# Folding the low rows of light experts by a 128-row product, and scattering their down projection unfolded

## The chip, the cores and the metric

One NeuronCore of a Trainium2 chip runs the whole program. The metric is the device time of one execution in microseconds; the time before is the median of three runs, 1436.17 us (1435.22 to 1437.19).

## The reference

A two-layer decoder trunk over 256 tokens of width 1024. Each layer has a mixer (window attention beside a state-space branch), then a feed-forward part: dense in the first layer, a mixture of experts in the second. The change touches the mixture alone.

```
def _swiglu(h, wg, wu, wd):
    return (jax.nn.silu(h @ wg) * (h @ wu)) @ wd

logits = x2d @ w_router                      # 256 tokens, 8 experts
top_v, top_i = lax.top_k(logits, 2)
gates = softmax(top_v)
# for each expert e, over the tokens that chose it:
#     y[tok] += _swiglu(x2d[tok], wg[e], wu[e], wd[e]) * gate
# widths: 1024 -> 3584 -> 1024
```

All values are float32.

## The kernel before

**Precision.** TensorE multiplies in a reduced 32-bit form. So each operand is split into a high part and the rest (`wh` and `wl` of a weight tile `w`, by ScalarE and then VectorE), and a product is the sum of several partial ones that accumulate in one bank of PSUM.

**Experts.** The eight experts are sorted by the number of their tokens. The four largest ("heavy", places 0 to 3) get 128 rows; the four smallest ("light", places 4 to 7) get `ROOM` = 64 rows. They run alternately, in the order 0, 4, 1, 5, 2, 6, 3, 7 (`TURNS`, line 30). Each expert has `NCH` = 7 chunks of 512 hidden columns, and each chunk loads 12 weight tiles of 512 KB: 4 for the gate, 4 for the up projection, 4 for the way down. A weight tile serves two products of 512 columns for each pair of parts.

**Heavy experts** (`glu_up`, `glu_down`) use three partial products: high x high, high x low, low x high.

**Light experts** (`light_up`, `light_down`) have at most 64 rows, so their high and low parts stand side by side in one 128-column set of weights: columns 0 to 63 are the high part, 64 to 127 the low part. Two products (with `wh` and with `wl`) then leave the sum for the high part in rows 0 to 63 of the bank and the one for the low part in rows 64 to 127. The result is the sum of the two halves. `join` (line 1407) forms it: ScalarE copies rows 64 to 127 to the tile `low`, and TensorE adds them to rows 0 to 63 by a product with `shift`, a 64x64 identity that lies in rows 64 to 127 of the place matrix tile `PTl`. A light chunk has two joins in the up projection (gate and up bank). After the last chunk of a light expert, `scatter_light` (line 1518) joins the two accumulators as well.

**From tokens to rows and back.** `gather_light` (line 1357) makes, for all light experts at once, the selection `PPl` (tokens by rows), uses it to pick the rows, and transposes it to the place matrix `PTl` (rows by tokens). `scatter` and `scatter_light` split an expert's result into `yh` and `yl` and hand them to `give` (line 1532), which multiplies the place matrix with both and adds the outcome, times the gate, to the residual `X`. The last expert is a light one, so its `scatter_light` and `give` are the end of the kernel: each half of `X` leaves for memory as soon as it is updated.

**Order.** The operations are recorded first, with the tiles that they read and write. A planner (`Plan.order`, line 240) then lays them out by list scheduling with costs written in the code, and the program is emitted in that order: each engine works through its own list, and weight loads stay in the order in which they were recorded. Buffers come in pools: 44 of 128x1024 (`m`: weight tiles, their splits, `yh`, `yl`, `PTl`), 8 of 128x512 (`h`: `low`, `sg`, `hth`, selections, place matrices), small ones (`s`), and 8 PSUM banks. A weight tile is loaded when a buffer of the first pool comes free, so products that end release loads. In the trace every operation has line 445, where they are emitted; they are told apart by their tiles, written as output, then inputs: `bank<-low,PTl` is the product of a join.

**The expert sort** (`sort`, line 1260) uses a 128x64 scratch tile `big` in the small pool, up to the two calls of `placed` that sort slots and gates.

Of the kernel before, what the change touches and what calls it, by code (L numbers as in the profile page):

```python
# [447 lines left out]
class Kernel:  # L448
# [811 lines left out]
    def sort(self, msk, ones):  # L1260

        nc, tt, ts, stt = self.nc, self.tt, self.ts, self.stt
        K = self.K
        bank = self.bank()
        for t in range(2):
            nc.tensor.matmul(bank[:, 0:8], ones, msk[:, 8 * t:8 * t + 8], start=t == 0, stop=t == 1)
        rows = self.S(8, "rows")
        nc.vector.tensor_copy(rows, bank[:, 0:8])
        key = self.S(8, "key")
        stt(key, rows, 8.0, K[:, CK:CK + 8], OP.mult, OP.add)  # L1270
        inner = lambda x: x.unsqueeze(1).to_broadcast([128, 8, 8])
        outer = lambda x: x.unsqueeze(2).to_broadcast([128, 8, 8])
        square = lambda x: x.rearrange("p (a b) -> p a b", a=8)
        big = self.big = self.S(64, "big")
        tt(square(big), inner(key), outer(key), OP.is_gt)
        place = self.S(8, "place")
        nc.vector.tensor_reduce(place, square(big), AX.X, OP.add)

        self.perm = self.S(64, "perm")
        tt(square(self.perm), inner(place), outer(K[:, CT:CT + 8]), OP.is_equal)  # L1280
        tt(square(big), square(self.perm), inner(K[:, CT:CT + 8]), OP.mult)
        at = self.S(8, "pi")
        nc.vector.tensor_reduce(at, square(big), AX.X, OP.add)
        ids = self.plan.buf("s", [128, 8], I32, "ids")
        nc.vector.tensor_copy(ids, at)
        self.known = len(self.plan.ops)
        self.plan.add("DMA", "registers", (None, ids, self.registers), {})
        self.sslot = self.placed(self.slot, "sslot")

        room = self.S(8, "room")  # L1290
        ts(room, place, float(HEAVY), float(128 - ROOM), OP.is_lt, OP.mult)
        ts(room, room, float(ROOM), None, OP.add)
        tt(rows, rows, room, OP.subtract)
        self.most = self.S(1, "most")
        nc.vector.tensor_reduce(self.most, rows, AX.X, OP.max)
        ts(self.most, self.most, 0.0, None, OP.max)
        self.over = self.S(16, "over")
        v = lambda x: x.rearrange("p (t e) -> p t e", t=2)
        tt(v(self.over), v(self.slot), room.unsqueeze(1).to_broadcast([128, 2, 8]), OP.subtract)
# [57 lines left out]
    def gather_light(self, hn):  # L1357

        nc = self.nc
        n = NE - HEAVY  # L1360
        m = n * ROOM
        PP = self.H("PPl", F32R)
        for t in range(2):
            for i in range(n):
                c, o = 8 * t + HEAVY + i, m * t + ROOM * i
                self.ts(PP[:, o:o + ROOM], self.K[:, CT:CT + ROOM], self.sslot[:, c:c + 1], None, OP.is_equal)
        h = [self.M("lx", F32R).rearrange("p (k e q m) -> p k e q m", k=2, e=n, q=2) for _ in range(4)]
        for b in range(4):
            bank = self.bank()
            for i in range(2):  # L1370
                k = 2 * b + i
                for j, x in enumerate(hn):
                    nc.tensor.matmul(bank[:, m * i:m * i + m], x[:, 128 * k:128 * k + 128], PP[:, m * (j // 2):m * (j // 2) + m], start=j == 0, stop=j == 3)
            for i in range(2):
                k = 2 * b + i
                hi, lo = (h[b][:, i, :, q] for q in range(2))
                v = bank[:, m * i:m * i + m].rearrange("p (e m) -> p e m", e=n)
                g = self.mg[:, k:k + 1]
                self.act(hi, v, AF.Copy, scale=g)
                self.stt(lo, v, g, hi.bitcast(F32), OP.mult, OP.subtract)  # L1380
        PT = self.M("PTl", F32R)
        for t in range(2):
            bank = self.bank()
            for i in range(n):
                o = m * t + ROOM * i
                nc.tensor.transpose(bank[0:ROOM, 128 * i:128 * i + 128], PP[:, o:o + ROOM].bitcast(F32), self.ident)
            nc.vector.tensor_copy(PT[0:ROOM, 512 * t:512 * t + 512], bank[0:ROOM])

        self.shift = PT[ROOM:128, 0:ROOM]
        nc.vector.tensor_copy(self.shift, self.ident[ROOM:128, ROOM:128])  # L1390
        bank = self.bank()
        for i in range(n):
            for t in range(2):
                o = m * t + ROOM * i
                nc.tensor.matmul(bank[0:ROOM, i:i + 1], PP[:, o:o + ROOM].bitcast(F32), self.rs[:, t:t + 1], start=t == 0, stop=t == 1)
        rs = self.S(4, "rsl")
        nc.vector.tensor_copy(rs[0:ROOM], bank[0:ROOM, 0:n])
        return PT[0:ROOM].rearrange("p (t e m) -> p t e m", t=2, e=n), lambda j, k: h[k // 2][:, k % 2, j].rearrange("p q m -> p (q m)"), rs[0:ROOM]

    def both(self, out, x, w, first):  # L1400

# [4 lines left out]

    def join(self, bank):

        low = self.H("low", F32R)[ROOM:128]
        self.act(low, bank[ROOM:128], AF.Copy)  # L1410
        self.nc.tensor.matmul(bank[0:ROOM], self.shift, low, start=False, stop=True, skip_group_check=True)
        return bank[0:ROOM]

    def light_up(self, src, of, rs):
# [31 lines left out]
    def moe(self, R):  # L1446
# [11 lines left out]
        for turn, j in enumerate(TURNS):  # L1458
            if j in GROUPS:
                self.plan.after = [mark] if j else []  # L1460
                got = self.gather(GROUPS[j], hn) if j < HEAVY else self.gather_light(hn)
                self.plan.after = []
                for n, i in enumerate(GROUPS[j]):
                    rows[i] = (n, *got)
            n, PT, of, rse = rows[j]
            acc = [self.bank(), self.bank()]
            for i in range(NCH):
                i == 0 and self.marks.append((f'e{j}', len(self.plan.ops) + 3))
                if i == self.gate_at - 1:
                    mark = len(self.plan.ops) + 1  # L1470
                if i == self.gate_at:
                    if j == 0:
                        hn = self.split_rows([mark])
                    mark = len(self.plan.ops) + 1
                if j:
                    w = [Late(lambda j=j, i=i, q=q: e[bass.ds(self.regs[j], 1), i, q].rearrange("o p n -> (o p) n")) for q in range(12)]
                else:
                    w = [e[0, i, q] for q in range(12)]
                self.ks = self.LEAN[1] if NCH * turn + i < self.LEAN[0] else self.KR[7]
                if j < HEAVY:  # L1480
                    ht = self.glu_up(w[:8], lambda t, k, n=n, of=of: of(n, k), 1, rse[:, n:n + 1])
                    down, scatter, to = self.glu_down, self.scatter, [acc]
                else:
                    ht = self.light_up(w[:8], lambda k, n=n, of=of: of(n, k), rse[:, n:n + 1])
                    down, scatter, to = self.light_down, self.scatter_light, acc

                if rest:
                    rest[0](*rest[1:])
                rest = (down, i, w[8:], ht, to, scatter(j, n, PT, acc) if i == NCH - 1 else None)
        rest[0](*rest[1:])  # L1490
        return hn

# [11 lines left out]
    def scatter(self, place, j, PT, acc):  # L1504

        y = []

        def half(h):
            if not y:
                y.extend((self.M("yh", F32R), self.M("yl", F32R)))  # L1510
            c = slice(512 * h, 512 * h + 512)
            self.act(y[0][:, c], acc[h], AF.Copy)
            self.tt(y[1][:, c], acc[h], y[0][:, c].bitcast(F32), OP.subtract)
            self.give(place, h, [[(PT[:, t, j], y[i][:, c]) for i in range(2)] for t in range(2)])

        return half

    def scatter_light(self, place, j, PT, acc):
        y = []

        def half(h):
            if not y:
                y.extend((self.M("yh", F32R), self.M("yl", F32R)))
            c = slice(512 * h, 512 * h + 512)
            a = self.join(acc[h])
            self.act(y[0][0:ROOM, c], a, AF.Copy)
            self.tt(y[1][0:ROOM, c], a, y[0][0:ROOM, c].bitcast(F32), OP.subtract)
            self.give(place, h, [[(PT[:, t, j], y[i][0:ROOM, c]) for i in range(2)] for t in range(2)])

        return half  # L1530

# [211 lines left out]
```

## Time and profile before

| | before |
|---|---|
| median of 3 runs | 1436.17 us |
| profiled execution, its own time | 1438.01 us |
| its span (first to last instruction) | 1436.0 us |
| TensorE busy | 1399.2 us, 97% |
| VectorE busy | 1204.7 us, 84% |
| ScalarE busy | 1013.6 us, 71% |
| DMA, mean rate | 294 GB/s |
| mean granted clock of TensorE | 0.989 |

The profile is of one execution. PE is TensorE's products and PEld its weight loads, which overlap; DVE is VectorE, ACT ScalarE, SP the engine that issues the loads. A busy TensorE is not one at its peak. The mixture takes roughly the second half: its loads start at about 412 us, the last of them lands at about 1410 us.

### The profile page before, as it was taken

What the parts mean: (1) busy time and instruction counts of PE and PEld (TensorE: products, weight loads), DVE (VectorE), ACT (ScalarE), POOL (GpSimd) and SP (SyncE); (2) the same over time, 40 slices, a digit from 0 to 9 for tenths busy, and PEclk for the clock granted to TensorE, in tenths of its full rate; (3) what the DMA queues carried; (4) which work ended last, traced back from release to release, by engine and by line L of the source; (5) the groups of instructions that cost most, each with busy time, mean ns of one, the idle gap of its engine ahead of it and who ended that gap; (6) DMA issues with size and microseconds to landing.
All of it is one profiled execution on the core that took longest, in us unless ns stands there. A gap on an engine that the chain in (4) does not pass through costs nothing.

```text
span 1436.0 us, 20731 instructions
## 1 busy us (share of the span) xinstructions
PE 1399.2 (97%) x6558; PEld 1070.7 (75%) x6558; DVE 1204.7 (84%) x1640; ACT 1013.6 (71%) x1322; POOL 25.4 (2%) x44
## 2 busy tenths in 40 slices
PE   7999999999999999999899999999999899999997
PEld 4888888888888878876678876678886667887554
DVE  7888994554695699899979999999898989998986
ACT  5586754445447387799778788988778778787775
POOL 3000110000000000000000000000000000000000
PEclk9999999999999899999999999999999999999999
DMA  6357155555447679699999999999999999999993
GB/s 218 106 171 241 57 163 191 177 189 187 140 147 258 241 235 375 219 363 383 357 354 382 383 392 363 394 348 393 378 377 374 371 408 355 378 388 394 405 395 122
DMA packets 116899, 422.57 MB, mean 294 GB/s; under 512 B 13360, under 2 KB 13872, under 8 KB 116784
## 3 DMA queue, kind: packets, MB, share of 16 engines
q1 hardware_dynamic: 116784, 421.20, 79.3%
q8 instruction: 53, 0.87, 0.2%
q14 instruction: 62, 0.51, 0.1%
HBM read 420.10 MB, written 1.05 MB: 293 GB/s over the span
## 4 chain that ended last, share of the span: by engine, by line
PE 88%; DVE 5%; DMA 2%; issue 2%; ACT 1%; SPq 0%; DVEq 0%; ACTq 0%
PE bank L445 88%; DVE wl L445 3%; DMA w<-in_moe_dram 2%; DVE X L445 1%; DMA w<-in_win_u_dram 1%; ACT wh L445 1%; ACT st L445 0%; SPq L445 0%; DVE ht L445 0%; DVE htl L445 0%; ACT xh L445 0%; DVE psm L445 0%; DVE xl L445 0%; DVE yl L445 0%; ACT sg L445 0%
## 5 line engine op out<-in xcount | busy, mean ns | idle before, releaser
L445 DVE TENSOR_TENSOR wl<-w,wh 128x1024 fp32r<-128x1024 f32 x758 | 884.3, 1219 | 90.9 <-ACT wh L445 59.2
L445 ACT ACTIVATE wh<-w 128x1024 fp32r<-128x1024 f32 x758 | 749.7, 1051 | 81.8 <-PE bank L445 32.2
L445 PE MATMUL bank<-wh,xh 128*128 128x512 f32 x448 | 174.1, 394 | 1.2 <-ACT wh L445 0.7
L445 PE MATMUL bank<-wl,xh 128*128 128x512 f32 x448 | 171.9, 393 | 0.7 <-DVE wl L445 0.6
L445 PE MATMUL bank<-wh,xl 128*128 128x512 f32 x448 | 171.5, 392 | 0.2 <-DVE xl L445 0.2
L445 PE MATMUL bank<-wl,lx 128*128 128x512 f32 x392 | 161.3, 416 | 6.1 <-DVE wl L445 5.8
L445 PE MATMUL bank<-wh,lx 128*128 128x512 f32 x392 | 155.0, 406 | 7.7 <-DVE ht L445 4.5
L445 PE MATMUL bank<-wh,hth 128*128 128x512 f32 x336 | 115.8, 399 | 0.0
L445 PE MATMUL bank<-wh,htl 128*128 128x512 f32 x336 | 114.4, 400 | 0.0
L445 PE MATMUL bank<-wl,hth 128*128 128x512 f32 x336 | 114.0, 397 | 0.0
L445 PEld LDWEIGHTS bank<-wl,lx 128*128 128x128 f32 x392 | 75.2, 192 | 42.2 <-DVE wl L445 20.2
L445 PEld LDWEIGHTS bank<-wl,xh 128*128 128x128 f32 x448 | 84.1, 188 | 21.4 <-DVE wl L445 3.8
L445 PEld LDWEIGHTS bank<-wh,xh 128*128 128x128 f32 x448 | 83.7, 188 | 20.3 <-ACT wh L445 2.5
L445 PEld LDWEIGHTS bank<-wh,xl 128*128 128x128 f32 x448 | 83.8, 188 | 17.8 <-DVE xl L445 0.6
L445 PEld LDWEIGHTS bank<-wh,lx 128*128 128x128 f32 x392 | 75.3, 192 | 24.8 <-ACT wh L445 4.1
L445 PE MATMUL bank<-wh,hh 128*128 128x512 f32 (+1 forms) x288 | 91.5, 385 | 0.4
L445 PE MATMUL bank<-wl,hh 128*128 128x512 f32 (+1 forms) x288 | 90.1, 381 | 0.0
L445 PE MATMUL bank<-wh,hl 128*128 128x512 f32 (+1 forms) x288 | 89.9, 380 | 0.0
L445 PE MATMUL bank<-wh,ht 128*128 128x512 f32 x224 | 88.4, 432 | 0.6 <-DVE ht L445 0.6
L445 PE MATMUL bank<-wl,ht 128*128 128x512 f32 x224 | 86.1, 414 | 1.4 <-DVE wl L445 1.3
L445 ACT ACTIVATE low<-bank 64x512 fp32r<-64x512 f32 x64 | 37.9, 594 | 52.4 <-PE bank L445 51.6
L445 PEld LDWEIGHTS bank<-wh,htl 128*128 128x128 f32 x336 | 62.6, 188 | 14.8 <-issue 1.9
(308 smaller groups left out, 1772.6 us busy)
## 6 DMA issues: line engine op xcount, KB each, us to landing
w<-in_moe_dram SPq DMA_DIRECT2D x672, 512.0 KB, 6.1
w<-in_dense_dram SPq DMA_DIRECT2D x84, 512.0 KB, 4.4
w<-in_wo_dram SPq DMA_DIRECT2D x16, 512.0 KB, 4.1
w<-in_win_u_dram SPq DMA_DIRECT2D x8, 512.0 KB, 5.1
w<-in_win_q_dram SPq DMA_DIRECT2D x8, 512.0 KB, 7.6
w<-in_win_kv_dram SPq DMA_DIRECT2D x4, 512.0 KB, 3.6
w<-in_wglu_dram SPq DMA_DIRECT2D x4, 512.0 KB, 3.7
X<-in_x_dram SPq DMA_DIRECT2D x2, 512.0 KB, 4.7
```

The source lines that it names most:

```text
L445: getattr(engines[o["eng"]], o["method"])(*map(real, o["a"]), **{n: real(v) for n, v in o["k"].items()})
```

## The change

The product of a join gets 128 rows: `fold` is a 128x64 tile of its own, the last 64 columns of the identity, with zeros in rows 0 to 63 and the identity in rows 64 to 127. `low` is now a copy of the whole bank.

The accumulators of the light experts are no longer joined. The place matrix `PTl` is written twice, to rows 0 to 63 and to rows 64 to 127, and light experts use the same `scatter` as heavy ones: `yh` and `yl` have 128 rows, and the product in `give` sums both halves. `scatter_light` is gone.

`big` moves from the small pool to one of the eight 128x512 buffers.

```diff
-        big = self.big = self.S(64, "big")
+        big = self.big = self.H("big")[:, 0:64]
...
-            nc.vector.tensor_copy(PT[0:ROOM, 512 * t:512 * t + 512], bank[0:ROOM])
-
-        self.shift = PT[ROOM:128, 0:ROOM]
-        nc.vector.tensor_copy(self.shift, self.ident[ROOM:128, ROOM:128])
+            for i in range(2):
+                nc.vector.tensor_copy(PT[ROOM * i:ROOM * i + ROOM, 512 * t:512 * t + 512], bank[0:ROOM])
+
+        self.fold = self.plan.buf("s", [128, ROOM], F32R, "fold")
+        nc.vector.tensor_copy(self.fold, self.ident[:, ROOM:128])
...
-        return PT[0:ROOM].rearrange("p (t e m) -> p t e m", t=2, e=n), lambda j, k: h[k // 2][:, k % 2, j].rearrange("p q m -> p (q m)"), rs[0:ROOM]
+        return PT.rearrange("p (t e m) -> p t e m", t=2, e=n), lambda j, k: h[k // 2][:, k % 2, j].rearrange("p q m -> p (q m)"), rs[0:ROOM]
...
-        low = self.H("low", F32R)[ROOM:128]
-        self.act(low, bank[ROOM:128], AF.Copy)
-        self.nc.tensor.matmul(bank[0:ROOM], self.shift, low, start=False, stop=True, skip_group_check=True)
+        low = self.H("low", F32R)
+        self.act(low, bank, AF.Copy)
+        self.nc.tensor.matmul(bank[0:ROOM], self.fold, low, start=False, stop=True, skip_group_check=True)
...
-                    down, scatter, to = self.light_down, self.scatter_light, acc
+                    down, to = self.light_down, acc
...
-                rest = (down, i, w[8:], ht, to, scatter(j, n, PT, acc) if i == NCH - 1 else None)
+                rest = (down, i, w[8:], ht, to, self.scatter(j, n, PT, acc) if i == NCH - 1 else None)
...
-    def scatter_light(self, place, j, PT, acc):
...
```

## Rows read from the trace of the kernel before

**Rows 1.** The page's busy times: us, share of the span, instructions.

```profile
PE 1399.2 (97%) x6558; PEld 1070.7 (75%) x6558; DVE 1204.7 (84%) x1640; ACT 1013.6 (71%) x1322; POOL 25.4 (2%) x44
```

**Rows 2.** Windows: length, busy us (count) of each engine, clock, DMA share, GB/s.

```profile
1185.00:1310.00 125.00, 124.92 (x556) 100.12 (x556) 115.76 (x110) 98.89 (x112) 0.00 (x0) 1.00 0.99 374
1310.00:1410.00 100.00, 95.65 (x355) 58.80 (x354) 88.38 (x89) 77.73 (x92) 0.00 (x0) 1.00 1.01 395
```

**Rows 3.** The chain that ended last, in time: start us, us, engine, tile.

```profile
881.00 60.97 PE bank L445 x262
...
950.74 160.61 PE bank L445 x696
...
1207.36 126.06 PE bank L445 x549
```

**Rows 4.** Groups by line: shapes, count | busy us, mean ns | idle before, releasers.

```profile
L445 ACT ACTIVATE low<-bank 64x512 fp32r<-64x512 f32 x64 | 37.9, 594 | 52.4 <-PE bank L445 51.6
...
L445 PE MATMUL bank<-low,PTl 64*64 64x512 f32 x64 | 28.3, 442 | 0.0
```

**Rows 5.** Timeline of weight loads around one join: start us, us, then idle before.

```profile
1108.33 0.19 PEld L445 LDWEIGHTS bank<-wh,lx 128*128 128x128 f32 x1
1108.87 0.13 PEld L445 LDWEIGHTS bank<-low,PTl 64*64 64x64 f32 x1 [0.35 <-issue]
1109.24 0.19 PEld L445 LDWEIGHTS bank<-wl,lx 128*128 128x128 f32 x1 [0.24 <-issue]
1109.34 0.19 PEld L445 LDWEIGHTS bank<-wh,lx 128*128 128x128 f32 x1
1109.58 0.19 PEld L445 LDWEIGHTS bank<-wl,lx 128*128 128x128 f32 x1
```

**Rows 6.** Timeline of weight loads with 128 rows and 64 columns.

```profile
589.92 0.19 PEld L445 LDWEIGHTS bank<-wl,hth 128*128 128x128 f32 x1
590.48 0.19 PEld L445 LDWEIGHTS bank<-fr_y,PPl 128*64 128x64 f32 x2 [0.36 <-issue]
...
655.88 0.56 PEld L445 LDWEIGHTS bank<-K,PPl 128*64 128x64 f32 x4
```

**Rows 7.** Timeline of weight loads around light `give` products, one group whole.

```profile
1100.67 0.19 PEld L445 LDWEIGHTS bank<-wh,hth 128*128 128x128 f32 x1
1101.22 0.18 PEld L445 LDWEIGHTS bank<-yl,PTl 64*128 64x128 f32 x1 [0.36 <-issue]
1101.65 0.19 PEld L445 LDWEIGHTS bank<-wh,lx 128*128 128x128 f32 x1 [0.24 <-issue]
1101.75 0.19 PEld L445 LDWEIGHTS bank<-wl,ht 128*128 128x128 f32 x1
...
1326.87 0.52 PEld L445 LDWEIGHTS bank<-yh,PTl 64*128 64x128 f32 x3 [0.35 <-PE bank L445]
```

**Rows 8.** The place matrix's copies (min/median/max ns, starts), and a window around them.

```profile
L445 DVE CAST PTl<-bank x2: 673/674/675, 691.8 to 714.2; 64x512 fp32r<-64x512 f32 x2
...
680.00:720.00 40.00, 35.07 (x147) 24.11 (x146) 36.28 (x46) 29.31 (x41) 0.00 (x0) 0.91 0.96 352
```

**Rows 9.** Timeline of the kernel's end.

```profile
1422.54 0.59 ACT L445 ACTIVATE low<-bank 64x512 fp32r<-64x512 f32 x1 [1.26 <-PE bank L445]
...
1424.89 0.59 ACT L445 ACTIVATE low<-bank 64x512 fp32r<-64x512 f32 x1 [0.30 <-PE bank L445]
...
1426.01 0.59 ACT L445 ACTIVATE yh<-bank 64x512 fp32r<-64x512 f32 x1 [0.53 <-PE bank L445]
...
1428.48 1.41 DVE L445 SCALAR_TENSOR_TENSOR X<-bank,sgt,X 128x512 f32<-128x512 f32 x2 [0.59 <-PE bank L445]
```

**Rows 10.** Windows around a wait of TensorE in a light stage.

```profile
1120.00:1125.00 5.00, 1.31 (x4) 0.64 (x3) 5.00 (x7) 5.00 (x6) 0.00 (x0) 0.74 1.02 409
1125.00:1130.00 5.00, 5.00 (x14) 3.90 (x14) 5.00 (x7) 2.17 (x3) 0.00 (x0) 0.58 0.98 359
```

**Rows 11.** The last readers of `big`: min/median/max ns, first and last start.

```profile
L445 DVE TENSOR_REDUCE sgt<-big x2: 213/216/220, 493.3 to 497.1; 128x8 f32<-128x64 f32 x2
```

More of the change, by code (lines that the diff above doesn't have):

```diff
@@ L1481, in moe @@
                     ht = self.glu_up(w[:8], lambda t, k, n=n, of=of: of(n, k), 1, rse[:, n:n + 1])
-                    down, scatter, to = self.glu_down, self.scatter, [acc]
+                    down, to = self.glu_down, [acc]
                 else:
                     ht = self.light_up(w[:8], lambda k, n=n, of=of: of(n, k), rse[:, n:n + 1])
-                    down, scatter, to = self.light_down, self.scatter_light, acc
+                    down, to = self.light_down, acc
                 if rest:
                     rest[0](*rest[1:])
-                rest = (down, i, w[8:], ht, to, scatter(j, n, PT, acc) if i == NCH - 1 else None)
+                rest = (down, i, w[8:], ht, to, self.scatter(j, n, PT, acc) if i == NCH - 1 else None)
         rest[0](*rest[1:])
@@ L1514, in half @@
             self.give(place, h, [[(PT[:, t, j], y[i][:, c]) for i in range(2)] for t in range(2)])
-        return half
-    def scatter_light(self, place, j, PT, acc):
[L1519 to L1528, printed above, removed]
         return half
```

## Prediction

> **What bounds the kernel now.** I read the busy shares first, then the same shares stage by stage, then the chain of work that ended last, and only then single instructions. The shares of the whole span put TensorE first: 1399.2 us of busy time out of 1436.0 [rows 1]. That share is a warning as much as an answer, because matmuls overlap and a stretched matmul also counts as busy. The windows by stage say more. While the last heavy expert runs (1185 to 1310 us), TensorE has no idle time worth naming (124.92 of 125 us), VectorE is busy for 93% of the stretch, and the loads flow at 374 GB/s [rows 2]. While the last light expert runs (1310 to 1410 us), TensorE is no longer full (95.65 of 100 us), VectorE is at 88%, and the loads run at 395 GB/s with the DMA engines at 1.01 [rows 2]. So three resources lie within about a tenth of each other: TensorE leads in the heavy stages, the loads lead in the last light one.
>
> The chain agrees. Between 881 and 1333 us three unbroken runs of TensorE alone make 60.97 + 160.61 + 126.06 = 347.6 of 452 us [rows 3]. A microsecond of TensorE work removed there can move the end; one removed after 1333 us can do so only behind the last load, in the tail.
>
> **The joins.** Each light chunk folds its two up-projection banks with `join`, and the last chunk of each light expert folds its two accumulators too: 4 x (14 + 2) = 64 joins, which is the count in both groups [rows 4]. One costs ScalarE a copy of 594 ns and TensorE a product of 442 ns as recorded [rows 4]. The recorded length is not the price on TensorE, as products overlap; the price is read from the starts of the weight loads. Around one join they start at 1108.33, 1108.87, 1109.24, 1109.34 and 1109.58 us [rows 5]: four steps in 1.25 us. An undisturbed step is 0.23 us (125 us over 556 products in the heavy stage [rows 2] give 0.225; the last step here is 0.24), so the surplus is 1.25 - 4 x 0.23 = 0.33 us. The rows show where the surplus sits: 0.35 us idle ahead of the 64x64 weight load and 0.24 us idle behind it, both put down to "issue", that is, to no semaphore [rows 5]. So a join costs TensorE 0.23 + 0.33 = 0.56 us.
>
> Eight joins go (two for each light expert). Two of them lie in the tail, below. The other six give TensorE 6 x 0.56 = 3.4 us, and ScalarE 6 x 0.594 us, which I price at nothing: ScalarE is busy 78 to 79% in these stages [rows 2].
>
> **The 56 joins that stay.** They become a product whose weights have 128 rows and 64 columns. Does the 0.33 us surplus vanish with the 64 rows? No instruction of this kernel has exactly the new form, so I bound it by its neighbours. The products of the row selection with the norm factors (`fr_y,PPl`) have 128 rows and 64 columns and are plain products: the weight load ahead of them starts at 589.92 us, theirs at 590.48 us, with 0.36 us idle put down to "issue" [rows 6]. That is the same gap as before a 64x64 load. The transposes of the same selection (`K,PPl`) also have 128 rows and 64 columns, and their weight loads follow with no idle time at all [rows 6]. The fold is a plain product, so I take the first: the surplus stays. The weight load itself grows from 0.13 us towards 0.19 us at most [rows 5], so 56 joins cost between nothing and 56 x 0.06 = 3.4 us more; two 64-column loads together took 0.19 us in [rows 6], so I take 0.4 us, near the lower end. The other end, no surplus at all, would give 56 x 0.33 = 18.5 us and is a rival below. ScalarE's copy now covers 128 partitions instead of 64 with the same 512 elements in each; copies of 128x512 out of a bank take what the 64x512 ones take (`yh` in the tail has 64 partitions and 0.59 us [rows 9], the `low` copies 594 ns [rows 4]), so I price it at nothing.
>
> Here a rule speaks against the change. The Trainium skill, page "TensorEngine Tiling (Array Packing)", section "Key Properties", says that a change of the tiling mode drains the engine, and its section "Available Configurations" lists 128x64 as a mode of its own beside 64x64 and 128x128. By that rule the 56 joins save nothing; if only the rows counted, they would save the 18.5 us. The gap ahead of `fr_y,PPl` agrees with the rule.
>
> **The way back to the tokens.** The light experts' `give` products have 64 rows now and 128 afterwards, the same shape as everything around them. Around one that stands alone the weight loads start at 1100.67, 1101.22, 1101.65 and 1101.75 us [rows 7]: three steps in 1.08 us, a surplus of 1.08 - 3 x 0.23 = 0.39 us. Seven groups of these products stand alone like this one ahead of the tail (the first is this one, the last at 1326.87 us [rows 7]); the rest sit beside another 64-row instruction and share its gap. The seven give 7 x 0.39 = 2.7 us. Their `yh` and `yl` cover 128 partitions instead of 64 with the same number of elements in each, which costs nothing more.
>
> **What is added.** Two more copies of the place matrix out of the bank, 0.67 us each on VectorE, where now there are two at 691.8 and 714.2 us [rows 8]. VectorE is 36.28 of 40 us busy there and TensorE idle for 4.93 us [rows 8], so part of 1.35 us can land on the path: ends 0 and 1.35 us, I take 0.7. The fold matrix is one copy of 128x64 in place of one of 64x64, among transposes and row selections: nothing. `big` moves to one of the eight half-width buffers. Its readers end at 497.3 us [rows 11], before the first chunk asks for its buffers, and only the selection and the place matrix share the pool there: nothing; without that cover a chunk's `sg` would wait until 497.3 us, once.
>
> **The tail.** Behind the last load everything is in series. The first accumulator is copied for its join at 1422.54 us, the second at 1424.89; its `yh` starts at 1426.01, the last two updates of `X` at 1428.48 [rows 9]. Without joins the second half's `yh` can start when its products end, and these end 0.56 us earlier, as the first join no longer sits between them: 1424.89 - 0.56 = 1424.3 instead of 1426.01, 1.7 us earlier. VectorE may have two `X` updates of the first half in the way (1.41 us for two [rows 9]). Ends 1.0 and 1.7 us; I take 1.5.
>
> **The sum.** TensorE gains 3.4 + 2.7 = 6.1 us ahead of the tail, spread over the stretch of those long runs. How much passes? Between nothing (VectorE or the loads are next in line at once) and everything. VectorE and the loads have about a tenth to spare in the heavy stages and less in the light ones, so I take six tenths: 3.7 us. Then -3.7 - 1.5 + 0.7 + 0.4 = -4.1 us. Against the profiled execution's own 1438.01 us (span 1436.0 and 2.0 around it) that is 1433.9; the median of the runs lies 1.84 us under that execution, so 1432.1, rounded to 1432.0 us.
>
> **Rivals.** (a) The middle gives nothing: VectorE, at 88 to 93%, is next in every stage, or the loads are. Only the tail's 1.5 us remain, against 1.1 us added: 1438.01 - 0.4 - 1.84 = 1435.8 us. For it speaks the last light stage, where TensorE already waits; against it the long unbroken runs of TensorE in the chain.
> (b) The 128-row fold really loses the gap. The first and the last light expert are held by VectorE and loads [rows 2, 8], so the 28 joins of the other two count: 28 x 0.33 = 9.2 us more on TensorE, at six tenths 5.5 us, with the 0.4 us above gone: 1432.1 - 5.9 = 1426.2 us (1422.5 if all of it passes). For it: the transposes without a gap; against it: the plain product with one. In the opposite case, which is my forecast, the change does not do the part that its title names.
> (c) Slower. TensorE, ahead of its splits, waits in one long piece and falls to the low clock. It happens now in the third light expert's stage: at 1120 us only 4 matmuls start in 5 us, the next 5 us see 14, and the granted clock is 0.74 and then 0.58 of 2.4 GHz, so partly at 1.2 GHz [rows 10]. Ten usual microseconds of a light stage hold 35 matmuls [rows 2], so this place costs (35 - 18) x 0.28 = 4.8 us. The order on each engine is worked out anew from the list of operations, and with 16 operations fewer and 2 more it can put a light expert's splits behind other work. It decides once TensorE stands as long as it does there, busy for 1.31 us of 5. If that takes the middle's gain and adds one such place: 1438.01 - 0.4 + 4.8 - 1.84 = 1440.6 us; two would give 1445.
>
> **How the numbers follow.** Forecast 0.43 (own range 1428.5 to 1434.0), (a) 0.26, (b) 0.09, (c) 0.22. About 0.2% (2.9 us) can be told from no change. Faster by more: most of the forecast and all of (b), 0.50. Within: (a) and the forecast's upper edge, 0.28. Slower by more: (c), 0.22. The range reaches down into (b) and up into (c), without the second stall: 1423 to 1442 us.
>
> **What would show it.** Weight loads of the fold with an idle gap of about 0.35 us ahead and 0.24 us behind, 56 of them. No gap around the light `give` products. The second half's `yh` in the tail about 1.7 us nearer to the last product. The forecast is wrong if the fold has no gap, if VectorE's busy share rises to the whole of a heavy stage, or if a new low-clock stretch appears.

## The result and the profile after

The changed kernel takes 1417.89 us (median of 4 runs, 1417.69 to 1418.63) against 1436.51 us before: a ratio of 0.9872, with a 95% interval of 0.9855 to 0.9889. That is 18.6 us, or 1.3%, faster. The forecast was 1432.0 us with a range of 1423 to 1442: the direction was right, the size was not, and the time lies below the range. A second comparison (experiment 9) gave 0.9863 (0.9843 to 0.9883). One execution of the kernel of experiment 10 took 1702.35 us at a granted clock of 0.75, where the others had 0.99, and is left out of what is said of that kernel.

In the page of the changed kernel, the busy times answer to [rows 1]. TensorE loses 25.2 us of busy time and VectorE nothing; the span goes from 1436.0 to 1415.9 us.

```profile
PE 1374.0 (97%) x6550; PEld 1073.1 (76%) x6550; DVE 1204.1 (85%) x1642; ACT 998.9 (71%) x1314; POOL 25.5 (2%) x44
```

The copies of the joins, by tile (durations are min/median/max, then first and last start), answer to [rows 4]: 56 copies of 128x512 at 597 ns, where 64 copies of 64x512 took 594 ns. So ScalarE does not pay for the wider copy, as priced, although both rows that the prediction named for this price are copies of 64 partitions.

```profile
L445 ACT ACTIVATE low<-bank x56: 577/597/604, 617.6 to 1395.3; 128x512 fp32r<-128x512 f32 x56
```

The timeline of weight loads around one fold answers to [rows 5], and here is the result in four lines:

```profile
634.28 0.19 PEld L445 LDWEIGHTS bank<-wh,lx 128*128 128x128 f32 x1
634.51 0.13 PEld L445 LDWEIGHTS bank<-low,fold 128*64 128x64 f32 x1
634.74 0.19 PEld L445 LDWEIGHTS bank<-wl,lx 128*128 128x128 f32 x1
634.97 0.19 PEld L445 LDWEIGHTS bank<-wh,lx 128*128 128x128 f32 x1
```

The loads start 0.23 us apart, through the fold as through anything else. The rows put no idle time ahead of the fold and none behind it; before, a join had 0.35 and 0.24 us [rows 5]. Over all joins, the median from the weight load ahead to the second one behind was 1.03 us and is 0.69 us.

The window answers to [rows 2]. In the last heavy stage VectorE is at 92% (96.86 of 105 us), where it was at 93%.

```profile
1185.00:1290.00 105.00, 104.83 (x475) 85.50 (x474) 96.86 (x92) 82.47 (x93) 0.00 (x0) 1.00 0.99 378
```

The tail, as a timeline, answers to [rows 9]. The first accumulator is copied at 1403.68 us, now straight to `yh`, and the last update of `X` ends at 1407.37 + 2.08 = 1409.45: 5.77 us. Before, it was 1422.54 to 1428.48 + 1.41 = 1429.89, 7.35 us. By the last update the tail is 1.6 us shorter; by the end of the span it is 1.2 us (1436.0 - 1422.54 = 13.46 us before, 1415.9 - 1403.68 = 12.22 us now).

```profile
1403.68 0.60 ACT L445 ACTIVATE yh<-bank 128x512 fp32r<-128x512 f32 x1 [1.43 <-PE bank L445]
...
1405.88 0.60 ACT L445 ACTIVATE yh<-bank 128x512 fp32r<-128x512 f32 x1 [1.60 <-PE bank L445]
...
1407.37 2.08 DVE L445 SCALAR_TENSOR_TENSOR X<-bank,sgt,X 128x512 f32<-128x512 f32 x3
```

### The profile page after: what moved, and what is told of

Its sections match the earlier page's. It is cut to its first block, busy times and chain, and to the rows that moved or that the text cites. A ratio compares the mean times of both kernels' runs of the same rounds, so it can differ in the third digit from the quotient of the medians.

```text
span 1415.9 us, 20663 instructions
## 1 busy us (share of the span) xinstructions
PE 1374.0 (97%) x6550; PEld 1073.1 (76%) x6550; DVE 1204.1 (85%) x1642; ACT 998.9 (71%) x1314; POOL 25.5 (2%) x44
## 4 chain that ended last, share of the span: by engine, by line
PE 85%; DVE 6%; DMA 3%; issue 3%; ACT 2%; SPq 0%; DVEq 0%; ACTq 0%
PE bank L445 85%; DVE wl L445 4%; DMA w<-in_moe_dram 3%; ACT wh L445 2%; DMA w<-in_win_u_dram 1%; DVE X L445 1%; ACT st L445 0%; SPq L445 0%; DVE ht L445 0%; DVE htl L445 0%; ACT xh L445 0%; DVE psm L445 0%; DVE xl L445 0%; ACT L445 0%; DVE yl L445 0%
## 5 line engine op out<-in xcount | busy, mean ns | idle before, releaser
L445 PEld LDWEIGHTS bank<-wh,hth 128*128 128x128 f32 x336 | 62.5, 188 | 14.0 <-issue 0.5
```

The costliest lines, as they stand in the source:

```text
L445: getattr(engines[o["eng"]], o["method"])(*map(real, o["a"]), **{n: real(v) for n, v in o["k"].items()})
```

## The experiments

The theory after the result (A): the gain is the idle gap around the 56 joins that stay. Against it stood two rivals: the unfolded way down brought it (B), or the new order of the whole program did (C). Experiments 1 to 3 take the change apart; 4 and 5 ask what makes the gap; 6 and 7 ask which stages pass it on; 8 to 10 go one step further. Times on different chips are compared by their ratios to the kernel before; a difference in ratio is turned into microseconds with 1436.5 us. The edits are shown against the changed kernel.

### 1. The fold alone

```diff
-            for i in range(2):
-                nc.vector.tensor_copy(PT[ROOM * i:ROOM * i + ROOM, 512 * t:512 * t + 512], bank[0:ROOM])
+            nc.vector.tensor_copy(PT[0:ROOM, 512 * t:512 * t + 512], bank[0:ROOM])
...
-                    down, to = self.light_down, acc
+                    down, scatter, to = self.light_down, self.scatter_light, acc
...
```

(`scatter_light` itself and the 64-row view of the place matrix are back as well.)

> The 128-row fold for all 64 joins, the accumulators of the light experts still joined, the place matrix with 64 rows as before. Theory A (the gain is the idle gap around the 56 remaining joins, 0.33 us each, which a 128-row product does not have): no idle time beside the weight loads of the fold; 64 x 0.33 = 21 us less on TensorE, of which those of the two middle light experts and those beside heavy experts pass; 11 to 15 us faster than before, about 1422 to 1425 us. Theory B (the gain came from the accumulators' way back): within 4 us of before, at least 1432 us. Theory C (the planner's new order brought most of it): no forecast for this kernel beyond a scatter of some us.

Measured: 1422.56 us, ratio 0.9904 (0.9878 to 0.993), 13.8 us faster. All 64 joins have the new form, and of the idle time ahead of everything that reads or writes `low` 0.2 us in all is put down to "issue" (16.1 us before):

```profile
L445 PEld LDWEIGHTS bank<-low,fold x64: 132/134/138, 620.2 to 1408.7; 128*64 128x64 f32 x64
...
  issue: 0.2, 1
```

The fold alone brings some seven tenths of the gain (13.8 of 18.4 to 19.7 us). Theory A holds, B falls.

### 2. The way down alone

```diff
-        nc.vector.tensor_copy(self.fold, self.ident[:, ROOM:128])
+        nc.vector.tensor_copy(self.fold[ROOM:128], self.ident[ROOM:128, ROOM:128])
...
-        low = self.H("low", F32R)
-        self.act(low, bank, AF.Copy)
-        self.nc.tensor.matmul(bank[0:ROOM], self.fold, low, start=False, stop=True, skip_group_check=True)
+        low = self.H("low", F32R)[ROOM:128]
+        self.act(low, bank[ROOM:128], AF.Copy)
+        self.nc.tensor.matmul(bank[0:ROOM], self.fold[ROOM:128], low, start=False, stop=True, skip_group_check=True)
```

> The up-projection joins with 64 rows as before (rows 64 to 127 of the same tile), the accumulators unfolded and scattered with the doubled place matrix. Theory A: the idle gap of 0.35 us ahead of each join is there as before; 8 joins and the gaps of give are gone, 4 to 7 us faster than before: 1429.5 to 1432.5 us. Theory B: 13 us faster or more, at most 1423 us.

Measured: 1432.22 us, ratio 0.9957 (0.994 to 0.9973), 6.2 us faster. The gap is back around the 56 joins, as this timeline of weight loads shows:

```profile
635.65 0.13 PEld L445 LDWEIGHTS bank<-low,fold 64*64 64x64 f32 x1 [0.35 <-issue]
636.01 0.19 PEld L445 LDWEIGHTS bank<-wl,lx 128*128 128x128 f32 x1 [0.24 <-issue]
```

The parts add up to 13.8 + 6.2 = 20.0 us against 18.4 to 19.7 us for the whole in its two comparisons.

### 3. Neither part, only what is added

This kernel combines the reversals of 1 and 2, but keeps the doubled place matrix, the moved `big` and the separate tile for the join's matrix. The second half of the place matrix is not read.

> Neither part: joins with 64 rows, accumulators joined; only what the change adds is there (two more copies of the place matrix, the scratch tile in another pool, a tile of its own for the join's matrix). Theories A and B: 0 to 1.4 us slower than before, 1436 to 1438 us. Theory C: the new order alone moves the time by 5 us or more.

Measured: 1435.77 us, ratio 0.9992 (0.9982 to 1.0002). No change that can be told from nothing, and nothing for theory C: an order worked out anew from a slightly different list moved the time by about 1 us. The two added copies of the place matrix cost nothing that shows. This kernel's profiled execution was its longest, 1442.34 us, so its time is read from the median.

### 4. Rows or columns

The join has both fewer rows and fewer columns than the products around it. Here its product has 64 rows and 128 columns, with zeros in the last 64. A second scratch tile (`perm`) moves in beside `big` to make room.

```diff
-        self.fold = self.plan.buf("s", [128, ROOM], F32R, "fold")
-        nc.vector.tensor_copy(self.fold, self.ident[:, ROOM:128])
+        self.fold = self.plan.buf("s", [128, 128], F32R, "fold")
+        for i in range(2):
+            nc.vector.tensor_copy(self.fold[ROOM:128, ROOM * i:ROOM * i + ROOM], self.ident[ROOM:128, ROOM * (1 - i):ROOM * (1 - i) + ROOM])
...
-        low = self.H("low", F32R)
-        self.act(low, bank, AF.Copy)
-        self.nc.tensor.matmul(bank[0:ROOM], self.fold, low, start=False, stop=True, skip_group_check=True)
+        low = self.H("low", F32R)[ROOM:128]
+        self.act(low, bank[ROOM:128], AF.Copy)
+        self.nc.tensor.matmul(bank, self.fold[ROOM:128], low, start=False, stop=True, skip_group_check=True)
```

> The changed kernel with a join product of 64 rows and 128 columns (the columns 64 to 127 are zeros, so the high half is left as it is) in place of 128 rows and 64 columns. If the rows decide the idle gap: 0.35 us ahead of each join and 0.24 us behind it are back, and the time is that of the down part alone, 1429 to 1433 us. If the columns decide it: no gap, 1417 to 1420 us.

Measured: 1432.6 us, ratio 0.9969 (0.9957 to 0.9982), and the gap is there:

```profile
635.54 0.18 PEld L445 LDWEIGHTS bank<-low,fold 64*128 64x128 f32 x1 [0.35 <-issue]
635.96 0.19 PEld L445 LDWEIGHTS bank<-wl,lx 128*128 128x128 f32 x1 [0.24 <-issue]
```

For products in the reduced 32-bit form the 64 rows make the gap; 64 columns with 128 rows do not.

### 5. The same fold as a plain float32 product

Why, then, did `fr_y,PPl` [rows 6], with 128 rows and 64 columns, have a gap? It is a plain float32 product. So the fold is made one, on the same tiles.

```diff
-self.nc.tensor.matmul(bank[0:ROOM], self.fold, low, start=False, stop=True, skip_group_check=True)
+self.nc.tensor.matmul(bank[0:ROOM], self.fold.bitcast(F32), low.bitcast(F32), start=False, stop=True, skip_group_check=True)
```

> The changed kernel with the fold taken as a plain float32 product (same tiles, read as float32) instead of the reduced 32-bit form. The prediction's neighbour with 128 rows and 64 columns that did show a gap, fr_y,PPl, is a plain float32 product with one column to stream. If the float32 form with 64 columns makes the gap: about 0.36 us idle ahead of each fold, and a product that costs about 0.2 us more for itself; 56 x 0.5 = 28 us more on TensorE, 1430 to 1438 us. If the gap of fr_y has another cause (its neighbours or its single column): no idle time ahead of the fold, only the longer product, 56 x 0.2 = 11 us more on TensorE, 1421 to 1426 us.

Measured: 1456.76 us, ratio 1.0134 (1.0117 to 1.0151). The gap ahead of the fold is back, with the shape unchanged:

```profile
639.87 0.19 PEld L445 LDWEIGHTS bank<-wh,lx 128*128 128x128 f32 x1
640.41 0.19 PEld L445 LDWEIGHTS bank<-low,fold 128*64 128x64 f32 x2 [0.35 <-issue]
641.41 0.19 PEld L445 LDWEIGHTS bank<-wl,lx 128*128 128x128 f32 x1 [0.81 <-DVE wl L445]
641.52 0.19 PEld L445 LDWEIGHTS bank<-wh,lx 128*128 128x128 f32 x1
...
641.99 0.42 PEld L445 LDWEIGHTS bank<-w,lx 128*128 128x128 f32 x2
642.64 0.19 PEld L445 LDWEIGHTS bank<-w,lx 128*128 128x128 f32 x1 [0.24 <-issue]
643.07 0.19 PEld L445 LDWEIGHTS bank<-w,lx 128*128 128x128 f32 x1 [0.24 <-issue]
```

The expectation had the mechanism and missed the size. From 639.87 to 641.52 us is 1.65 us, where the changed kernel takes 0.69 us (634.28 to 634.97): 0.96 us for each fold, not 0.5. That makes 56 x 0.96 = 54 us of TensorE work; the time rose by 37.6 us over the changed kernel (1.0134 - 0.9872), 70% of it. The 0.81 us behind the fold is not a wait for VectorE, though the line names it: 53 of the 56 folds have 0.81 us there, whatever tile comes next.

The last three lines show where most of the 0.96 us comes from. One of the twelve weight tiles of a light chunk is not split, and its two products (`w,lx`) are plain float32 with 128x128 weights. Each such product has two records 0.43 us apart (642.64 to 643.07), 0.86 us instead of the 0.23 us of a reduced one, so 0.63 us more; the 0.2 us of the expectation came from no row. The fold as a float32 product has two records as well; if it is as long, 0.96 - 0.63 = 0.33 us is left for the gap (an estimate), which is the price of a 64-row join. And the first `w,lx` load has no idle time ahead: float32 alone makes no gap, it takes the 64 columns too. The 0.24 us between the later ones, put down to "issue", is the longer product and no standstill.

### 6 and 7. Which stages pass the gain on

The fold is used for two of the four light experts, the 64-row join for the other two; the rest is the changed kernel.

```diff
+                    self.wide = j in (5, 6)        # experiment 7: (4, 7)
                     ht = self.light_up(w[:8], lambda k, n=n, of=of: of(n, k), rse[:, n:n + 1])
...
-        low = self.H("low", F32R)
-        self.act(low, bank, AF.Copy)
-        self.nc.tensor.matmul(bank[0:ROOM], self.fold, low, start=False, stop=True, skip_group_check=True)
+        low, r = self.H("low", F32R), slice(0 if self.wide else ROOM, 128)
+        self.act(low[r], bank[r], AF.Copy)
+        self.nc.tensor.matmul(bank[0:ROOM], self.fold[r], low[r], start=False, stop=True, skip_group_check=True)
```

> The 128-row fold only for the two middle light experts (places 5 and 6), 64-row joins for the first and the last (places 4 and 7); the rest as in the changed kernel. Theory A with the prediction's view of the stages (the first and last light expert are held by VectorE and loads): nearly the whole gain of the fold is here, 1417 to 1421 us. If every stage passes its share: half of the fold's gain, about 1424 us.

> The mirror image: the 128-row fold only for places 4 and 7. With the prediction's view of the stages: little of the fold's gain, 1426 to 1431 us. If every stage passes its share: about 1424 us.

Measured: 1423.82 us, ratio 0.9915 (0.9893 to 0.9937), with the fold in the middle two; 1424.49 us, ratio 0.991 (0.9892 to 0.9929), with the fold in the first and the last. Against the way down alone (0.9957) each half brings 6.0 and 6.8 us, each to within about 4 us. The view that the first and last light expert would give little is wrong. The windows from 620 to 680 us, which lie within the first light expert, show why. With the 64-row join there (first line, experiment 6) TensorE is busy for 58.57 us and VectorE for 57.00 us; with the fold (second line, experiment 7) VectorE is busy for 59.36 us, and 245 products run instead of 234.

```profile
620.00:680.00 60.00, 58.57 (x234) 40.48 (x234) 57.00 (x56) 53.48 (x64) 0.00 (x0) 1.00 1.00 387
```

```profile
620.00:680.00 60.00, 58.59 (x245) 42.47 (x243) 59.36 (x58) 53.80 (x67) 0.00 (x0) 1.00 1.02 404
```

With the fold VectorE is nearly full here (99%); without it, it was not yet (95%).

The traces also show how the gain splits. The table has the time from the first `low` copy of each light expert to that of the next one, heavy expert included, and for the last one to the end of the span, in us.

| from light expert | way down alone (2) | fold in the middle two (6) | fold in the first and last (7) | changed kernel |
|---|---|---|---|---|
| first | 228.9 | 228.9 | 223.3 | 224.1 |
| second | 230.4 | 223.9 | 230.4 | 224.9 |
| third | 228.0 | 226.1 | 228.1 | 226.1 |
| last | 125.6 | 125.6 | 123.1 | 123.2 |

The fold's 14 joins of one light expert are worth 14 x 0.33 = 4.6 us of TensorE work. Some 5 us come out in the first, 6 in the second, 2 in the third and 2.5 in the last. Each column is one execution, and the stretches at the low clock differ among them, so a microsecond or two of a difference can be theirs.

### 8 to 10. The last 64-row products of a light chunk

The transposes of `sg` in `light_up` still have 64 rows. Here they take all 128; rows 64 to 127 carry numbers that nobody reads.

```diff
-        nc.vector.tensor_copy(rs[0:ROOM], bank[0:ROOM, 0:n])
+        for i in range(2):
+            nc.vector.tensor_copy(rs[ROOM * i:ROOM * i + ROOM], bank[0:ROOM, 0:n])
...
-        h = self.H("sg")[0:ROOM]
+        h = self.H("sg")
...
-            self.nc.tensor.transpose(bank[:, ROOM * i:ROOM * i + ROOM], h[:, 128 * i:128 * i + 128], self.ident[0:ROOM, 0:ROOM])
-        b = bank[:, :4 * ROOM].rearrange("p (k m) -> p k m", k=4)
+            self.nc.tensor.transpose(bank[:, 128 * i:128 * i + 128], h[:, 128 * i:128 * i + 128], self.ident)
+        b = bank.rearrange("p (k m) -> p k m", k=4)[:, :, 0:ROOM]
```

(`join` returns the whole bank, and the norm factors are returned for all 128 rows.)

> The changed kernel with the last 64-row products of the light experts widened as well: the transposes of sg take all 128 rows (the lower 64 are not used afterwards), so no instruction of a light chunk has 64 rows. Theory A: the idle time put down to issue ahead of and behind these transposes goes, 0.14 to 0.24 us for each of some 34 groups, 5 to 8 us of TensorE; 2 to 5 us faster than the changed kernel, 1413 to 1416 us. If VectorE and the loads now hold every stage: the same as the changed kernel within 2 us.

> The changed kernel itself, beside the next one on the same chip: 1416 to 1420 us, a ratio of 0.985 to 0.989.

> The kernel with the widened transposes of sg, beside the changed kernel on the same chip. If the gaps of the last 64-row products still carry time: 2 to 5 us faster than the changed kernel. If VectorE and the loads hold the stages now: within 2 us of it, and the earlier 3 us were the difference of two chips.

Measured first: 1414.46 us, ratio 0.9848 (0.9832 to 0.9864). Then beside the changed kernel on one chip: the changed kernel 1418.9 us, ratio 0.9863 (0.9843 to 0.9883); this one 1413.2 us, ratio 0.9829 (0.9813 to 0.9846). Both comparisons put it ahead, by 3.4 and 4.9 us in ratio, with intervals that overlap a little. On the one chip the executions themselves do not overlap: 1413.09 to 1414.38 us against 1417.13 to 1421.29 us. So it is very likely faster than the changed kernel, by 3 to 5 us. The transposes in the changed kernel (first fence) and here (second), as timelines of weight loads:

```profile
643.18 0.32 PEld L445 LDWEIGHTS bank<-K,sg 64*128 64x128 f32 x4 [0.35 <-issue]
```

```profile
657.50 0.59 PEld L445 LDWEIGHTS bank<-K,sg 128*128 128x128 f32 x4
```

The four loads take longer, 0.59 us instead of 0.32, but nothing stands still ahead of them; from the load ahead to the second one behind it is about 0.90 us instead of 1.04.

## Why the prediction failed, step by step

**The bound.** Right. Work taken from TensorE moved the end: 70% of the 54 us added in experiment 5 came out at the end, and 12.2 to 13.5 us of the fold's 18.5 us (the changed kernel's two ratios against 0.9957), 66 to 73%. The prediction's six tenths were about right as a mean; by the table of experiments 6 and 7 the first two light experts passed the whole of the fold's gain and the last two about half.

**The price of a join, 0.33 us beyond its own step.** Right: 0.34 us vanished (1.03 to 0.69 us in the medians), with the 0.35 and 0.24 us of idle time.

**The 56 joins that stay.** This is the step that failed. It asked whether the gap belongs to the 64 rows, found two neighbours with 128 rows and 64 columns, and took `fr_y,PPl`, which has the gap, over `K,PPl`, which has none, because the fold is a plain product like the first and not a transpose. The difference that counted was another one: `fr_y,PPl` is a float32 product, and the fold multiplies in the reduced form. Experiment 5 shows it with the same tiles and shape. The trace of before had a third neighbour that the prediction left out: `w,lx`, plain float32 with 128 columns and without a gap ahead (from 621.95 us on). With it in view, float32 alone could not explain the gap of `fr_y,PPl`, and with `K,PPl` the 64 columns alone could not either. (Not every operand is split, as the paragraph on precision has it: this tile is multiplied whole.) The term was put at +0.4 us and was 18.5 us of TensorE work in the other direction. With 56 x 0.33 at six tenths, 11.1 us, the prediction's own sum would have been 1432.1 - 0.4 - 11.1 = 1420.6 us, 2.7 us from the median.

The Trainium skill's rule, page "TensorEngine Tiling (Array Packing)", sections "Key Properties" and "Available Configurations", was read to mean that 128x64 is a mode whose change drains the engine. The runs agree for 64 rows (experiments 2 and 4) and for a plain float32 product with 64 columns (experiment 5); for the reduced form with 64 columns they do not, and there the measurement decides. Why the reduced form is spared is not shown.

**Rival (b)** named what happened and gave it 0.09. Even so its time, 1426.2 us, was 8 us too high: it let only the 28 joins of the middle light experts count; all 56 would have made it 1420.6 us. The window that excluded the first light expert [rows 8] covers its last 40 us, in which the rows for the next expert are also picked and TensorE waits. In the 60 us ahead of it TensorE was busy throughout, 60.00 us, and VectorE for 57.06 us:

```profile
620.00:680.00 60.00, 60.00 (x242) 41.73 (x241) 57.06 (x55) 54.58 (x65) 0.00 (x0) 1.00 1.00 379
```

That one window was read as the whole stage.

**The way down.** Right. Without the fold's 0.4 us the prediction's terms give 3.7 + 1.5 - 0.7 = 4.5 us; experiment 2 measured 6.2 us (3.9 to 8.6). Ahead of the tail, the loads of `give` products now start like their neighbours'. The tail was put at 1.5 us and is 1.6 us by the last update, 1.2 us by the end of the span. Its sign, the second half's `yh` 1.7 us earlier, came out smaller: from the first copy it took 3.47 us (1422.54 to 1426.01) and takes 2.20 us (1403.68 to 1405.88), 1.3 us less.

**What is added.** 0.7 us was a small overestimate or nothing: experiment 3 is within its interval of no change. `big` in a half-width buffer cost nothing that shows.

**Rival (c), a new wait with the low clock,** did not come as a loss, although one of its signs did: the granted clock falls for a short stretch at 940 us (0.66 over five microseconds, TensorE busy for 3.75 of them), where it did not before. The mean granted clock rose all the same, from 0.989 to 0.993. The place like [rows 10] is still there, in the third light expert's stage at 1095 us, with 25 products in ten microseconds where there were 18, and a granted clock of 0.79 and 0.86 of 2.4 GHz, so partly at 1.2 GHz:

```profile
1095.00:1100.00 5.00, 2.59 (x8) 1.60 (x7) 5.00 (x7) 4.47 (x7) 0.00 (x0) 0.79 1.01 402
1100.00:1105.00 5.00, 5.00 (x17) 3.35 (x17) 4.63 (x5) 1.23 (x3) 0.00 (x0) 0.86 1.01 392
```

**The chances.** The gap was a yes-or-no question worth up to 18.5 us, and it rested on one neighbour that differed from the fold in a property that was never listed. With two neighbours that contradict each other, 0.09 was too little, and the range had to reach the end that one of them stood for.

## What to carry to other kernels

Idle time of TensorE put down to "issue" on both sides of a small product can be a price that its length doesn't show: here 0.33 us for a product of 0.23 us, paid 64 times. Compare the starts of the loads with those of an undisturbed stretch, for a longer product leaves such idle time too. Padding a 64-row product with zero rows to 128 cost nothing that shows on any engine here, and removed it. When an operation's cost is read from a neighbour, write down every property in which the two differ, the number format too, before choosing between neighbours that disagree. And a window speaks for its own microseconds, not for the whole stage.

## What the runs showed of the hardware

Whether a product amid reduced 128x128 ones makes TensorE stand still depended on rows, columns and number format together. Reduced 32-bit form: 64x64 and 64x128 (rows x columns) gave 0.35 us ahead and 0.24 us behind, 128x64 gave none. Plain float32: 128x64 gave 0.35 us ahead, 128x128 none; one product of 128x64 weights with 512 columns took 0.96 us more than the same in the reduced form. Float32 transposes: 64x128 gave 0.35 us ahead (`sg` in the changed kernel), 128x128 none (experiment 8), 128x64 none [rows 6].
